# Attention pieces in a fixed TensorE order beside the projections, key norms beside the query projection, adaLN sums by token tile

## The chip, the cores and the metric

The kernel runs on one core of a Trainium2 chip. The metric is the device time of one execution in microseconds (us), as the median over runs. One further execution was taken by the profiler; all views of the profile belong to that one.

## The reference

One layer of a diffusion backbone: 256 latent tokens and 256 context tokens of width 2048, one neighbourhood attention of 16 heads of 128, and a gated ConvFFN of width 5504. Cut to what is computed:

```python
sh1, sc1, g1, sh2, sc2, g2 = adaln(c, w_ada, b_ada)        # silu(c) @ w_ada + b_ada, six vectors of 2048
csh1, csc1, ... = adaln(c_ctx, w_ada, b_ada)
h  = modulate(rms_norm(x,   norm_mix_g), sh1,  sc1)
hc = modulate(rms_norm(ctx, norm_mix_g), csh1, csc1)
q, k, v = split(concat(h, hc) @ w_qkv)                     # q of the latent tokens alone
q, k = rms_norm(q, q_g), rms_norm(k, k_g)                  # per head
p = softmax(q k^T * scale + bias(rpb), masked by window)   # 256 queries x (256 latent + 256 context) keys
x = x + g1 * ((p v) @ w_o)
hf = modulate(rms_norm(x, norm_ffn_g), sh2, sc2)
gate, up = split(dwconv3(hf @ w_up, conv_w, conv_b))
out = x + g2 * ((silu(gate) * up) @ w_down)
```

All inputs are float32. To keep that precision every operand of a large product is split into a high part, rounded to a faster format, and a low part (the rest); a product is then three matmuls: high by high, high by low, low by high.

## The kernel before

**Weights.** Every weight tile is 256 rows by up to 512 columns. `wpair` (line 147) loads it on SP's queue (tile wr, four buffers), casts it on ScalarE into wh (three buffers, line 155) and subtracts on VectorE into wl (two buffers, line 156). `weight` (line 185) keeps two pairs ahead, in the order of one list for the whole kernel.

**First products.** While the first third of adaLN is formed on TensorE, the first keys and the values of groups 0 and 1 are accumulated (`first_products`, line 459).

**The attention phase.** The 16 heads are worked in four groups of four. Projections of 512 columns follow each other: query 0, key 1, query 1, value 2, key 2, query 2, key 3, query 3, value 3. `project` (line 383) takes eight weight pairs; for each it calls `nat` (line 370), which runs over two token tiles (queries) or four (keys and values, which also cover the context), with six matmuls for each token tile. The results stand in the four PSUM banks pj.

Two lists of pieces of work are fed in beside them. `side` holds attention pieces and is ticked after each token tile in `nat` at RATE = 0.46 or RATE3 = 0.36 pieces; `ada` holds the later adaLN parts and is ticked after each weight pair, at 0.44 times the number of token tiles.

- A **score piece** (line 600): three matmuls into a bank, bias add and row maximum on VectorE, exponential on ScalarE, reciprocal on VectorE, scaling on ScalarE. There are two for each head, one for each query tile.
- A **turn** (line 627): four transposes of the probabilities into a bank, cast on ScalarE (high part), subtraction on VectorE (low part).
- A **weigh** (line 641): 12 matmuls of 256 columns with the values, and a copy on ScalarE.
- **Key and query norms** (`norm_transpose`, line 515; `split_k`, `split_q`): for each token tile four squares with sums on ScalarE, a power -0.5 on GpSimd with Newton steps on VectorE (`rsqrt_newton`, line 192), the product on VectorE, four transposes, and a split on ScalarE and VectorE. Keys have four token tiles, queries two. Before, they are traced between a query projection's end and the next key or value projection.
- An **adaLN part** (`ada_tasks`, line 252): a 512 KB load of two 128-row blocks on SP's queue (tile wa, three buffers); five of eight parts are scaled on ScalarE (line 276) and added on GpSimd (line 277), the others are done on VectorE (line 279). After eight parts `finish` (line 283) adds both sums on VectorE, transposes four blocks on TensorE and reduces. There are 12 columns of eight parts in this phase, for g1, sh2 and gs2.

**Order.** Each engine takes its instructions in one fixed order, which a scheduler sets when the kernel is built, from its own model of the times. So TensorE's order is what that model found ready, across projections, attention, norms and adaLN. SP's queue, with all loads, is in order too. The scores, norms and weighings alternate between the bank pairs ms and mx (`at`, line 83); turns use ms alone.

**After it.** The output product (line 740 on) starts with the first 12 heads' rows, with the rest of group 3's attention beside it, then comes the feed-forward part. `xg` there reads the last adaLN columns.

Of the kernel before, what the change touches and what calls it, by code (L numbers as in the profile page):

```python
# [15 lines left out]
P = 128  # L16
# [12 lines left out]
RATE, RATE3 = 0.46, 0.36  # L29
# [21 lines left out]
def block_kernel(  # L51
# [29 lines left out]
    turns = []  # L81
# [47 lines left out]
    rp = cp.tile([NH * NDR, 31], F32, name="rp")  # L129
    nc.scalar.dma_start(rp, rpb)  # L130
# [121 lines left out]
    def ada_tasks(pool, i, c, dst, gcol=None):  # L252
# [29 lines left out]

        def finish():
            acc = st["acc", 0]
            nc.vector.tensor_add(acc, acc, st["acc", 1])
            sp = ms()
            for b in range(4):
                nc.tensor.transpose(sp[:, b * P : (b + 1) * P], acc[:, b * P : (b + 1) * P], ident)
            d = dst[:, 4 * c : 4 * c + 4]
            bc = S_B + i * KD + 4 * c  # L290
            nc.vector.tensor_reduce(
                out=d, in_=sp.rearrange("p (b t) -> p b t", t=P), axis=AX.X, op=ALU.add
            )
# [7 lines left out]
        return [(lambda q=q: load(q), lambda q=q: part(q)) for q in range(KD // KT)], finish  # L301

    def ada_pieces(cols):

        loads = [l for pairs, _ in cols for l, _ in pairs]
        parts = [p for pairs, _ in cols for _, p in pairs]
        n = KD // KT

        def piece(i):
# [5 lines left out]
            if i % n == 1 and i > n:  # L315
                cols[i // n - 1][1]()
            with tc.issue_after(last[0]), tc.issue_after(last[1]):
                if i < len(parts):
                    parts[i]()
                else:  # L320
                    cols[-1][1]()

# [14 lines left out]
    xp = xctx.enter_context(tc.tile_pool(name="xp", bufs=1))  # L337
    s32 = xp.tile([P, KD, 32], F32, name="s32")
# [31 lines left out]
    def nat(psl, tt0, w, kt0, n, first, last):  # L370

        wh, wl = w
        for i, pt in enumerate(psl):
            ts = slice((tt0 + i) * P, (tt0 + i + 1) * P)
            for k in range(n):
                kt = kt0 + k
                a, z = first and k == 0, last and k == n - 1
                nc.tensor.matmul(pt, hh[:, kt, ts], wh[:, k, :], start=a, stop=False)  # L378
                nc.tensor.matmul(pt, hh[:, kt, ts], wl[:, k, :], start=False, stop=False)  # L379
                nc.tensor.matmul(pt, hl(kt, ts), wh[:, k, :], start=False, stop=z)  # L380
# [131 lines left out]
    def row2k(name):  # L512
        return ap.tile([P, CH], F32, tag="r2", name=name, bufs=3)

    def norm_transpose(pt, gcol, dh, dl, t0):

        ss = ap.tile([P, 4], F32, tag="ss", name="ss", bufs=2)
        qn = row2k("qn")
        for h in range(4):
            hc = slice(h * HD, (h + 1) * HD)  # L520
            nc.scalar.activation(qn[:, hc], pt[:, hc], AF.Square, accum_out=ss[:, h : h + 1])
        nc.vector.tensor_scalar(
            out=ss, in0=ss, scalar1=1.0 / HD, scalar2=EPS, op0=ALU.mult, op1=ALU.add
        )
        r = rsqrt_newton(ap, ss, 4, "n")
        nc.vector.tensor_tensor(
            out=qn.rearrange("p (h d) -> p h d", d=HD), in0=pt.rearrange("p (h d) -> p h d", d=HD),
            in1=r.unsqueeze(2).to_broadcast([P, 4, HD]), op=ALU.mult,
        )
        tp = at()  # L530
        for h in range(4):
            nc.tensor.transpose(tp[:, h * P : (h + 1) * P], qn[:, h * HD : (h + 1) * HD], ident)
        tpv = tp.rearrange("p (h t) -> p h t", t=P)
        nc.scalar.activation(dh[:, :, t0 : t0 + P], tpv, AF.Copy, scale=gcol)
        nc.vector.scalar_tensor_tensor(
            out=dl[:, :, t0 : t0 + P], in0=tpv, scalar=gcol,
            in1=dh[:, :, t0 : t0 + P].bitcast(F32), op0=ALU.mult, op1=ALU.subtract,
        )

    def split_k(kps):  # L540
        kh = kv.tile([P, 4, 2 * T], F32R, tag="kh", name="kh")
        kl = kv.tile([P, 4, 2 * T], F32R, tag="kl", name="kl")
        for tt in range(4):
            norm_transpose(kps[tt], kg, kh, kl, tt * P)
        return kh, kl

    def split_q(qps):
        qq = kv.tile([P, 2, 4, T], F32R, tag="qq", name="qq")
        qh, ql = qq[:, 0], qq[:, 1]
        for tt in range(2):  # L550
            norm_transpose(qps[tt], qg, qh, ql, tt * P)
        return qh, ql

    def split_v(vps, g):
        vv = (big, ap)[g % 2 == 0].tile([P, 2, 4, CH], F32R, tag=("vv", "row1")[g % 2], name="vv")
        vh, vl = vv[:, 0], vv[:, 1]
        for tt in range(4):
# [4 lines left out]
        return vh, vl  # L562
# [27 lines left out]
    def attention(g, q, k, v):  # L590

        (qh, ql), (kh, kl) = q, k

        bank = lambda: ms() if late else at()

        def head(h4):
# [3 lines left out]
            def scores(qt):  # L600
                with tc.high_priority():
                    if qt == 0:
# [3 lines left out]
                        st["ph"] = kv.tile([P, 4, T], F32R, tag="pth", name="pth", bufs=2)  # L606
                        st["pl"] = ap.tile([P, 4, T], F32R, tag="ptl", name="ptl", bufs=2)
                    tq = slice(qt * P, (qt + 1) * P)
                    sp = bank()
                    nc.tensor.matmul(sp, qh[:, h4, tq], kh[:, h4, :], start=True, stop=False)  # L610
                    nc.tensor.matmul(sp, qh[:, h4, tq], kl[:, h4, :], start=False, stop=False)
                    nc.tensor.matmul(sp, ql[:, h4, tq], kh[:, h4, :], start=False, stop=True)
# [14 lines left out]
            def turn(qt):  # L627
                tq = slice(qt * P, (qt + 1) * P)
                pr, tp = st[qt], ms()
                for kt in range(4):  # L630
                    nc.tensor.transpose(
                        tp[:, kt * P : (kt + 1) * P], pr[:, kt * P : (kt + 1) * P], ident
                    )
# [7 lines left out]
            def weigh():  # L641
                (vh, vl), ph, pl, op = v[0], st["ph"], st["pl"], bank()
                hc = slice(h4 * HD, (h4 + 1) * HD)
                for kt in range(4):
                    nc.tensor.matmul(
                        op[:, :T], vh[:, kt, hc], ph[:, kt, :], start=(kt == 0), stop=False
                    )
                    nc.tensor.matmul(op[:, :T], vh[:, kt, hc], pl[:, kt, :], start=False, stop=False)
                    nc.tensor.matmul(
                        op[:, :T], vl[:, kt, hc], ph[:, kt, :], start=False, stop=(kt == 3)  # L650
                    )
# [8 lines left out]
        s = [[lambda f=h[0], t=t: f(t) for t in range(2)] for h in heads]  # L660
        t = [[lambda f=h[1], t=t: f(t) for t in range(2)] for h in heads]
        w = [[h[2]] for h in heads]
        seq = s[0] + t[0] + s[1] + t[1]
        if g == 3:
            return [seq, w[0] + s[2] + t[2] + w[1] + s[3] + w[2] + t[3] + w[3]]
        return [seq + w[0] + s[2] + w[1] + t[2] + s[3] + w[2] + t[3] + w[3]]

    cols = [ada_tasks(ap, 2, c, g1T) for c in range(4)]
    cols += [ada_tasks(ap, 3, c, sh2T) for c in range(4)]
    cols += [ada_tasks(ap, 4, c, gs2T, S_GF) for c in range(4)]  # L670
    ada.extend(ada_pieces(cols))

    v, v1 = [[split_v([vsums[g][:, tt, :] for tt in range(4)], g)] for g in range(2)]
    kw, qw = [
# [284 lines left out]
```

## Time and profile before

| what | us |
|---|---|
| median of 3 runs | 1446.48 |
| lowest, highest | 1446.38, 1448.18 |
| the profiled execution | 1445.85 |
| its span, first to last instruction | 1444.0 |

A page of the profile gives the busy time of each engine: PE is TensorE's matmuls, PEld its weight loads, DVE VectorE, ACT ScalarE, POOL GpSimd, SP the queue that issues the loads. A row of a group names the line of the kernel, the engine, what is written from what, the count, the busy us and the mean ns of one, and after the bar the idle time of the engine just before them with what ended it. A row of a timeline has the start in us, the duration, and merged neighbours as "x2" and so on; idle time before it stands in brackets. A row of waits has the total us, how often, and the longest.

### The profile page before, as it was taken

To read this page: it belongs to the slowest core of one execution; us is meant where nothing else is said; L and a number is where in the kernel's file an instruction comes from. 1 tells how busy PE (TensorE), PEld (TensorE's weight loads), DVE (VectorE), ACT (ScalarE), POOL (GpSimd) and SP (SyncE) were. 2 spreads that over 40 slices of the span, in tenths; PEclk is the share of its full clock that TensorE was granted. 3 is DMA by queue.
4 is the path that set the end of the run, shared out by engine and by line. 5 is a ranking of instruction groups with operands and counts; after the bars stand their busy time and mean duration, and the time that the engine had idled before them with its cause. 6 is when DMAs were issued, how large, how long until landed. Compare 5 with 4: busy or idle time off the path is not lost.

```text
span 1444.0 us, 21091 instructions
## 1 busy us (share of the span) xinstructions
PE 1399.1 (97%) x7608; PEld 1167.8 (81%) x7608; DVE 1000.0 (69%) x1541; ACT 778.5 (54%) x1356; POOL 281.1 (19%) x208
## 2 busy tenths in 40 slices
PE   5999999999999999999899999999999999999998
PEld 2666787877787887888788888888888888888888
DVE  4556687686868768756768787887877775545454
ACT  4322265775555675755556566665666654333333
POOL 1000025465445555300101111111111000000000
PEclk9999999999999999999899999999999999999999
DMA  9999548687677677545567777777776666566554
GB/s 308 357 333 313 190 125 269 206 259 218 214 219 254 215 239 232 178 138 189 174 201 224 237 230 242 236 229 234 228 240 196 182 175 206 182 207 204 172 173 156
DMA packets 208920, 317.14 MB, mean 220 GB/s; under 512 B 23360, under 2 KB 87744, under 8 KB 208816
## 3 DMA queue, kind: packets, MB, share of 16 engines
q1 hardware_dynamic: 208688, 315.79, 70.4%
q8 instruction: 59, 0.97, 0.3%
q14 instruction: 45, 0.37, 0.1%
q10 hardware_dynamic: 128, 0.01, 0.0%
HBM read 312.75 MB, written 3.01 MB: 219 GB/s over the span
## 4 chain that ended last, share of the span: by engine, by line
PE 74%; issue 9%; DMA 5%; DVE 4%; ACT 3%; POOL 2%; SPq 1%; DVEq 0%; POOLq 0%; ACTq 0%
PE pj L727 18%; PE pj L733 9%; PE mx L727 8%; PE ms L727 7%; PE pj L379 5%; PE pj L378 5%; PE pj L380 5%; PE mx L733 4%; PE ms L733 4%; DMA wa<-in_w_ada 3%; PE ms L411 2%; PE mx L378 2%; PE mx L379 2%; PE mx L380 2%; POOL acc L277 2%
## 5 line engine op out<-in xcount | busy, mean ns | idle before, releaser
L156 DVE TENSOR_TENSOR wl<-wr,wh 128x1024 fp32r<-128x1024 f32 (+2 forms) x425 | 503.8, 1186 | 280.6 <-PE pj L733 106.3
L155 ACT CAST wh<-wr 128x1024 fp32r<-128x1024 f32 (+2 forms) x425 | 412.1, 971 | 428.8 <-PE pj L727 135.1
L277 POOL TENSOR_TENSOR acc<-acc,wa 128x512 f32<-128x512 f32 x144 | 223.6, 1553 | 428.8 <-issue 260.1
L379 PE MATMUL pj<-wl,hh 128*128 128x512 f32 x512 | 204.7, 400 | 3.5 <-DVE wl L156 3.4
L380 PE MATMUL pj<-wh,hl 128*128 128x512 f32 x512 | 201.7, 397 | 0.0
L378 PE MATMUL pj<-wh,hh 128*128 128x512 f32 x512 | 194.4, 400 | 2.5 <-ACT hh L450 2.5
L727 PE MATMUL pj<-hf,wh 128*128 128x512 f32 x688 | 176.3, 396 | 2.0 <-DVE hf L819 2.0
L727 PEld LDWEIGHTS pj<-hf,wh 128*128 128x128 f32 x688 | 124.9, 191 | 25.1 <-DVE hf L819 2.8
L276 ACT ACTIVATE wa<-wa,sT 128x512 f32<-128x512 f32 x144 | 97.4, 718 | 74.5 <-DMA wa<-in_w_ada 69.3
L379 PEld LDWEIGHTS pj<-wl,hh 128*128 128x128 f32 x512 | 97.7, 191 | 27.2 <-DVE wl L156 6.3
L378 PEld LDWEIGHTS pj<-wh,hh 128*128 128x128 f32 x512 | 96.8, 190 | 26.9 <-issue 3.4
L380 PEld LDWEIGHTS pj<-wh,hl 128*128 128x128 f32 x512 | 97.5, 191 | 19.5
L733 PEld LDWEIGHTS pj<-hf,wl 128*128 128x128 f32 x688 | 94.6, 192 | 6.8
L733 PE MATMUL pj<-hf,wl 128*128 128x256 f32 x688 | 97.8, 285 | 0.0
L727 PE MATMUL mx<-hf,wh 128*128 128x512 f32 x352 | 97.7, 394 | 0.0
L727 PE MATMUL ms<-hf,wh 128*128 128x512 f32 x336 | 90.9, 390 | 0.0
L279 DVE SCALAR_TENSOR_TENSOR acc<-wa,sT,acc 128x512 f32<-128x512 f32 x80 | 73.7, 921 | 6.9 <-DMA wa<-in_w_ada 6.3
L727 PEld LDWEIGHTS ms<-hf,wh 128*128 128x128 f32 x336 | 63.1, 188 | 14.2
L727 PEld LDWEIGHTS mx<-hf,wh 128*128 128x128 f32 x352 | 60.6, 190 | 7.8
L478 DVE TENSOR_TENSOR vsum<-vsum,mx 128x512 f32<-128x512 f32 x64 | 43.2, 684 | 34.2 <-PE mx L380 34.0
L733 PEld LDWEIGHTS mx<-hf,wl 128*128 128x128 f32 x352 | 53.7, 189 | 7.1 <-DVE wl L156 0.4
L584 POOL TENSOR_TENSOR bt<-bt,maskt 128x384 f32<-128x384 f32 x16 | 17.9, 1123 | 206.4 <-DMA bt<-rpd 173.7
(251 smaller groups left out, 2212.0 us busy)
## 6 DMA issues: line engine op xcount, KB each, us to landing
wr<-in_w_up SPq DMA_DIRECT2D x160, 512.0 KB, 4.5
wa<-in_w_ada SPq DMA_DIRECT2D x128, 512.0 KB, 4.6
wr<-in_w_qkv SPq DMA_DIRECT2D x93, 512.0 KB, 4.8
wr<-in_w_down SPq DMA_DIRECT2D x63, 512.0 KB, 4.8
wx<-in_w_ada SPq DMA_DIRECT2D x56, 512.0 KB, 8.6
wr<-in_w_o SPq DMA_DIRECT2D x24, 512.0 KB, 3.9
wr<-in_w_down SPq DMA_DIRECT2D x45, 256.0 KB, 3.0
wr<-in_w_up SPq DMA_DIRECT2D x16, 384.0 KB, 3.4
```

What stands on the lines that cost most here:

```text
L155: a = nc.scalar.copy(hi[:, :kn, :cn], w[:, :kn, :cn])
L156: b = nc.vector.tensor_tensor(out=lo[:, :kn, :cn], in0=w[:, :kn, :cn], in1=hi[:, :kn, :cn].bitcast(F32), op=ALU.subtract,)
L276: nc.scalar.mul(w[:, k, :], w[:, k, :], s)
L277: nc.gpsimd.tensor_add(acc, acc, w[:, k, :])
L279: nc.vector.scalar_tensor_tensor(out=acc, in0=w[:, k, :], scalar=s, in1=acc, op0=ALU.mult, op1=ALU.add)
L378: nc.tensor.matmul(pt, hh[:, kt, ts], wh[:, k, :], start=a, stop=False)
L379: nc.tensor.matmul(pt, hh[:, kt, ts], wl[:, k, :], start=False, stop=False)
L380: nc.tensor.matmul(pt, hl(kt, ts), wh[:, k, :], start=False, stop=z)
L411: nc.tensor.matmul(ap_[32 * k : 32 * k + 32, :n], s32[:, 4 * q + k, :], w[:, k * n : (k + 1) * n], start=(q == 0), stop=(q == 3), tile_pos ...
L478: nc.vector.tensor_add(acc[:, h0 + i, :], acc[:, h0 + i, :], pr_[i])
L727: nc.tensor.matmul(pts[b][:, : t1 - t0], wh[:, k, bs], mov(kt, slice(t0, t1)), start=(kt == 0 and t0 == 0), stop=False,)
L733: nc.tensor.matmul(pts[b][:, :T], wl[:, k, bs], mov(kt, slice(0, T)), start=False, stop=(kt == kn - 1),)
```

## The change

`pin` is new: it ties an instruction behind the one traced before it on its engine, so that the scheduler can't move it. All matmuls and transposes of `nat`, of the attention pieces, of the norms and of adaLN are pinned in this phase; so TensorE's order there is the order of the program text. The other engines' orders are still the scheduler's.

The norms become two kinds of pieces, `norm` (squares to product, in place) and `flip` (transposes and split); the splitting of values becomes pieces too. `project` gets a list of pieces, spreads it evenly over its token tiles, and ends when the list is empty. The lists are written out by hand: S, T and W are scores, turn and weigh, with head and query tile. Key norms and flips stand in the query projection that follows their projection; query norms and flips at the head of the next key or value projection.

The adaLN parts are ticked after each token tile, 0.125 (query projections) or 0.56 of a part, and start after the first query projection. The sum of both halves (`total`) is taken one part after a column's last, its transposes three parts later. Their banks alternate as the others do.

Further: turns use both bank pairs; four row buffers (r2) instead of three; queries of every group are copied out of PSUM into them; the bias table's source `rp` is loaded later, from another pool; the output product's side pieces tick at 512/400 instead of 512/340, and its sum tile `sacc2` takes over a key buffer.

```diff
-RATE, RATE3 = 0.46, 0.36
+ADA_RATE = {2: 0.125, 4: 0.56}
...
+    def pin(ins):
+        if pinned:
+            tc.keep_in_program_order(ins)
...
+        def total():
+            nc.vector.tensor_add(st["acc", 0], st["acc", 0], st["acc", 1])
+
         def finish():
             acc = st["acc", 0]
-            nc.vector.tensor_add(acc, acc, st["acc", 1])
-            sp = ms()
+            sp = bank()
...
             if i % n == 1 and i > n:
                 cols[i // n - 1][1]()
+            if i % n == 4 and i > n:
+                cols[i // n - 1][2]()
...
             side.tick(side.rate)
-    def project(c0, nt):
+            ada.tick(ada.rate)
+
+    def project(c0, nt, pieces=(), lead=0):
         psl = [pj() for _ in range(nt)]
+        side.extend(pieces)
+        for _ in range(lead):
+            side.popleft()()
+        side.rate = len(side) / (nt * (KD // KT))
+        side.credit = 0.5
+        ada.rate = ADA_RATE[nt]
         for kt in range(0, KD, KT):
             nat(psl, 0, weight(w_qkv, kt, KT, c0, CH), kt, KT, kt == 0, kt == KD - KT)
-            ada.tick(0.44 * nt)
+        side.drain()
+        side.rate = ada.rate = 0.0
         return psl
...
-                pr, tp = st[qt], ms()
+                pr, tp = st[qt], bank()
...
+    kn, kt_, k = norms(out_of_psum(kps, kw), kg, k_slots)
+    pieces = mix(v1[:3], kn[:3]) + [v1[3], kt_[0], kn[3]] + kt_[1:]
+    qs = out_of_psum(project(0, 2, pieces))
...
+    ada.extend(ada_pieces(cols))
+    for g in range(4):
+        qn, qt, q = norms(qs, qg, q_slots)
+        heads = attention(g, q, k, values[g])
+        if g == 0:
+            pieces = mix(qn, v0[:2]) + v0[2:] + qt
+        else:
+            pieces = qn + qt
+        c0 = (g + 1) * CH
         if g == 3:
+            pieces += heads("S00 S01 S10 T00 S11 T01 S20 T10 S21 T11")
+            vps = project(2 * D + g * CH, 4, pieces)
+            for piece in split_v(vps, g, values[g]):
+                piece()
+            rest = heads("W0 T20 S30 T21 W1 S31 W2 T30 T31 W3")
+            break
+        pieces += heads("S00 S01 S10 T00 S11 T01 S20 T10 W0 T11 S21 T20 W1 S30")
         if g == 1:
+            n = len(pieces) // 2
+            vps = project(2 * D + c0, 4, pieces[:n])
+            pieces = split_v(vps, 2, values[2]) + pieces[n:]
         if g == 2:
+            kw = big.tile([P, 4, CH], F32, tag="row1", name="kw")
+        kps = project(D + c0, 4, pieces, 5 if g == 1 else 0)
+        kn, kt_, k = norms(out_of_psum(kps, kw), kg, k_slots)
+        a, b = heads("T21 S31 W2 T30"), heads("T31 W3")
+        pieces = mix(kn[:2], a[:2]) + [kn[2], kt_[0], a[2], kn[3], kt_[1], a[3], kt_[2]]
+        pieces += [b[0], kt_[3], b[1]]
+        qs = out_of_psum(project(c0, 2, pieces, 1))
+    pinned.clear()
...
-            tick = (lambda: side.tick(cn / 340)) if i == 0 else (lambda: ada.tick(1.0))
+            tick = (lambda: side.tick(cn / 400)) if i == 0 else (lambda: ada.tick(1.0))
```

More of the change, by code (lines that the diff above doesn't have):

```diff
@@ L512, in row2k @@
     def row2k(name):
[L513 to L538, printed above, removed]
@@ new lines, in block_kernel, with out_of_psum, mix @@
+    kw = oT[:, 8:16, :].rearrange("p (t a) c -> p t (a c)", t=4)
+    def out_of_psum(pts, dst=None):
+        out = [dst[:, tt, :] if dst is not None else row2k("qw") for tt in range(len(pts))]
+        for o, pt in zip(out, pts):
+            nc.scalar.copy(o, pt)
+        return out
+    def mix(*lists):
+        return [p for row in zip(*lists) for p in row]
+    pinned.append(True)
+    values = [{} for _ in range(4)]
+    v0, v1 = [
+        split_v([vsums[g][:, tt, :] for tt in range(4)], g, values[g]) for g in range(2)
+    ]
```

176 lines of the change are left out of this document (88 added, 88 removed).

## The prediction

> **What bounds the kernel now.** I read the page's busy times first, then the windows, then TensorE's timeline where a window lost time, then the waits.
>
> ```profile
> span 1444.0 us, 21091 instructions
> PE 1399.1 (97%) x7608; PEld 1167.8 (81%) x7608; DVE 1000.0 (69%) x1541; ACT 778.5 (54%) x1356; POOL 281.1 (19%) x208
> 193.45:601.00 407.55, 391.40 (x1872) 320.50 (x1871) 308.29 (x466) 256.68 (x537) 207.40 (x143) 0.99 0.73 228
> 300.00:330.00 30.00, 25.54 (x129) 20.60 (x128) 25.57 (x43) 24.23 (x76) 17.60 (x13) 1.00 0.78 243
> 360.00:380.00 20.00, 17.28 (x85) 13.76 (x85) 15.77 (x21) 10.62 (x19) 6.14 (x5) 1.00 0.62 194
> 380.00:436.00 56.00, 56.00 (x281) 47.05 (x280) 40.80 (x58) 34.73 (x75) 26.89 (x21) 1.00 0.73 222
> 436.00:458.00 22.00, 18.81 (x74) 14.56 (x73) 19.82 (x25) 12.69 (x24) 13.50 (x9) 0.84 0.77 251
> 458.00:536.00 78.00, 78.00 (x386) 64.95 (x385) 55.40 (x87) 52.32 (x115) 38.84 (x27) 1.00 0.76 237
> 536.00:557.00 21.00, 18.09 (x86) 14.40 (x85) 18.36 (x32) 15.24 (x46) 15.77 (x11) 0.92 0.71 224
> 557.00:599.00 42.00, 42.00 (x199) 34.80 (x198) 27.36 (x50) 22.00 (x37) 21.42 (x15) 1.00 0.78 236
> ```
>
> Columns of a window: its length, then busy us and instructions of PE, PEld, DVE, ACT and POOL, then TensorE's granted clock, the DMA share and GB/s. TensorE sets the end. The change works in 193.45 to 601 us, from the first query product to the first matmul of the output product. Some windows there are full; four are not (300, 360, 436 and 536), and two of those also show a reduced clock. In them VectorE is busy 79 to 90% of the time, in the full ones 65 to 73%.
>
> Busy time hides part of the loss, because ends of matmuls are modelled. So I price TensorE by the spacing of starts:
>
> ```profile
> 433.93 0.39 PE L378 MATMUL pj<-wh,hh 128*128 128x512 f32 x1
> 434.15 0.39 PE L379 MATMUL pj<-wl,hh 128*128 128x512 f32 x1
> 434.38 0.39 PE L380 MATMUL pj<-wh,hl 128*128 128x512 f32 x1
> 434.61 0.60 PE L532 MATMUL mx<-ident,qn 128*128 128x128 f32 x4
> 434.96 0.71 PE L378 MATMUL pj<-wh,hh 128*128 128x512 f32 x2
> ...
> 316.18 0.28 PE L649 MATMUL ms<-pth,vv 128*128 128x256 f32 x1
> 316.30 0.28 PE L645 MATMUL ms<-pth,vv 128*128 128x256 f32 x1
> ...
> L379 PE MATMUL pj<-wl,hh 128*128 128x512 f32 x448 | 178.9, 399 | 3.5 <-DVE wl L156 3.4
> L631 PE MATMUL ms<-ident,pr 128*128 128x128 f32 x112 | 17.3, 274 | 1.6 <-ACT pr L624 1.4
> L532 PE MATMUL ms<-ident,qn 128*128 128x128 f32 x48 | 7.4, 276 | 4.8 <-DVE qn L526 2.7 <-ACT kh L534 1.3 <-DVE gs2T L291 0.8
> L288 PE MATMUL ms<-ident,acc 128*128 128x128 f32 x48 | 7.3, 274 | 0.0
> L645 PE MATMUL mx<-pth,vv 128*128 128x256 f32 x24 | 7.0, 292 | 2.1 <-ACT pth L635 2.1
> L610 PE MATMUL ms<-kh,qq 128*128 128x512 f32 x14 | 5.8, 418 | 0.1
> L379 PE MATMUL mx<-wl,hh 128*128 128x512 f32 x14 | 5.5, 391 | 0.0
> ```
>
> A 512-column matmul takes 0.227 us of the queue, four transposes 0.355, a 256-column matmul 0.118. Each of the last rows is one of a family of equal rows (projections L378 to L380, scores L610 to L612, weighing L645, L648 and L649, and two banks, ms and mx). So the range holds 3 x 448 = 1344 projection matmuls and 3 x 14 = 42 left from the first products (314 us), 6 x 14 = 84 score matmuls (19), 6 x 24 = 144 of 256 columns (17) and 112 + 96 + 48 = 256 transposes (23): 373 us of 407.55, so **34.2 us are lost**. By the same count the full windows from 380, 458 and 557 lose 0.8, 1.9 and 0.8 us of 176, which is 2%, and the four bad ones 6.2, 3.9, 7.3 and 5.8, together 23.2 of 93. A floor of 2% on 373 is 7.5 us, so at most 34.2 - 7.5 = **26.7 us** can be won.
>
> What the losses are made of:
>
> ```profile
> 449.64 0.63 PE L532 MATMUL ms<-ident,qn 128*128 128x128 f32 x4 [1.14 <-DVE qn L526]
> 451.76 0.79 PE L379 MATMUL pj<-wl,hh 128*128 128x512 f32 x1 [1.50 <-DVE wl L156]
> 452.36 0.63 PE L380 MATMUL pj<-wh,hl 128*128 128x512 f32 x1
> 452.78 0.63 PE L378 MATMUL pj<-wh,hh 128*128 128x512 f32 x1
> ...
> PE mx L532 <- DVE qn L526: 2.5, 2, 1.7
> ```
>
> TensorE's queue is in order; a transpose of normalized keys stands ahead of ready matmuls and waits for the norm. After two waits of at most 1.5 us the spacing is 0.43 us instead of 0.227: the clock has halved. The Trainium skill (TensorE: Matmul & The Clock Gate, section HAM oscillation) asks only for no idle gap over about 3.4 us; this trace halves below that, and the trace decides. Half clock makes 0.16 x 22 + 0.08 x 21 = 5.2 of the bad windows' 23.2 us (22%). By the page the short waits that I leave below would cost no clock, and my sum would be about 2 us lower.
>
> TensorE's waits for norms, keys, probabilities and adaLN are 4.8 + 2.5 + 2.1 + 1.6 = 11.0 us (rows of L532 on ms, L532 on mx, L645, L631); those for weight splits 3.5 (L379). So about 24% of the 23.2 us belongs to splits, **5.6 us**, and the other 17.6 to pieces that stand too close behind what they read.
>
> **The change part by part.**
>
> *Fixed TensorE order.* No matmul is removed; two score groups (6 x 0.227 = 1.4 us) move from the output product into the last value product, which is nothing in the sum. A projection of 4 token tiles has 32 slots of six matmuls (1.36 us), a query projection 16. In the first key projection 22 pieces share 32 slots, 1.45 slots each, so the transpose of head 0 comes three pieces behind its scores, 5.9 us plus two score groups, 7.3 us. What lies between, from the rows below, is a reduce (0.69), a scaling (0.72), an exponential of the same size, a bias add of half of it and small steps: some 3 us bare, and 4 us are left for queues. The tightest is the query transpose in the third key projection: 18 pieces on 32 slots put it after 5 slots, 6.8 us; the norm's ACT, POOL and DVE steps need 4 to 6 us there. I take the 17.6 us as gone; next in line are the splits.
>
> ```profile
> L619 DVE TENSOR_REDUCE nm<-ms 128x1 f32<-128x512 f32 x14 | 9.6, 687 | 0.3
> L624 ACT ACTIVATE pr<-pr,rs 128x512 f32<-128x512 f32 x28 | 19.7, 721 | 5.6 <-DVE rs L623 5.6
> L195 POOL TENSOR_TENSOR nr<-ss,mhalf 128x4 f32<-128x4 f32 x21 | 25.6, 1221 | 28.5 <-DVE ss L522 26.5 <-DVE nt L196 1.0 <-ACT wh L155 0.9
> L156 DVE TENSOR_TENSOR wl<-wr,wh 128x1024 fp32r<-128x1024 f32 x74 | 104.4, 1412 | 20.5 <-PE pj L379 13.6 <-ACT oT L653 2.9 <-ACT wa L276 1.5
> L276 ACT ACTIVATE wa<-wa,sT 128x512 f32<-128x512 f32 x108 | 73.2, 719 | 74.5 <-DMA wa<-in_w_ada 69.3 <-DVE acc L279 1.7 <-POOL acc L277 1.4
> L277 POOL TENSOR_TENSOR acc<-acc,wa 128x512 f32<-128x512 f32 x108 | 166.7, 1543 | 99.5 <-ACT wa L276 53.3 <-DVE acc L274 17.7 <-ACT wh L155 13.5
> 474.42 0.37 SPq L139 DMA_DIRECT2D wa<-in_w_ada  x1
> 495.38 0.37 SPq L139 DMA_DIRECT2D wa<-in_w_ada  x1
> ...
> DMA to landing us min/median/max: 3.5/4.7/8.7
> ```
>
> *Key norms beside the query projection.* Each needs one POOL power (1.22 us); now these queue behind adaLN adds (1.54 each) that wait for loads. In a query projection (21.8 us of matmuls, 27.8 with its pieces) only two adaLN parts remain of seven, so that chain shortens. The query projection's 27.8 us are 96 x 0.227 = 21.8, seven transpose groups (2.5), two weighings of 12 x 0.118 (2.8) and one score group (0.7). In it VectorE has eight splits of 1.41 (11.3 us), twelve passes over 512 columns at some 0.7 by the reduce's row (four norms, four key splits, three probability splits, one score; 8.4) and an estimated 3 of small steps: 23 us, 82%, about what the bad windows have. VectorE's whole work stays 308 us: 76% of the phase now, 78% over 393 us, 81% if all were won. Splits have two buffers, so one can be made only once TensorE has left the one before: a late norm on VectorE delays the next split. I raise the splits' 5.6 us by half to **8.4** (bounds: 2.8 if shorter chains halve it, and 21 if the bad windows' 25% spreads over the 83 us of three query projections).
>
> *adaLN sums by token tile.* 0.25 parts a step in query projections instead of 0.88, 2.24 instead of 1.76 in the others: 17.9 parts in a key or value projection of 48 to 54 us, so one per 2.7 to 3.0 us. Three buffers carry them. The two SP rows are the first and last of 8 loads, spaced 3.0 us while TensorE was full, and ScalarE waited for many of these loads already (69.3 us over the phase). SP is in order, so a load that waits for a buffer holds the next weight load, and a waiting ACT scale holds the next weight cast. The five projections' TensorE work is 5 x 43.6 of matmuls, 27 score groups (18.4), 38 transpose groups (13.5) and 6 weighings (8.5): 258 us, with the floor 264. At 3.0 us a part each wants 53.8 us; the two with 14 and 13 pieces and the one with nine last 48 to 50.5 and fall short by some 9 us together. Half of it can be made up in the query projections, so I take **4 us** (bounds: 0, and the slow rival). The two parts left over run in the output product, which is busy on TensorE.
>
> *At nothing:* squares written to a small tile, products in place and a fourth row buffer (no engine time); two more ScalarE copies of 512 columns, under 0.72 us each, for the third group's queries (ScalarE is 63% busy); transposes over four banks instead of two; the bias table's later load, which has the first products to hide behind. The first query projection can no longer run among the last first products: 0 to 2 us, taken as inside the 4.
>
> Sum: 1445.85 (the profiled execution; span 1444.0 and 1.85 around it) - 26.7 + 8.4 + 4 = 1431.6. The median of the runs is 0.6 above that execution: **1432 us**.
>
> **The rivals.**
>
> *Nearly all is won:* no wait but the 2% floor; 1446.5 - 26.7 = 1420. For it: 78 us in a row at that floor with VectorE at 71%. Against: VectorE must then run at 81%.
>
> *The waits change names:* the order on TensorE is fixed, that on the other engines isn't, so a norm may still come late, or the splits do. With the bad windows' 25% lost over the first query projection and the three later ones (106 us) it is 26 us, the whole gain: 1446, in a band of 1441 to 1449. For it: every window with VectorE over 79% lost time.
>
> *adaLN loads become the bound, slower:* the place is the five key and value projections. If a part takes 3.3 us there (a 4.7 us landing, two scales, two adds, a queue, over three buffers), they last 89.6 x 3.3 = 296 us instead of 264, and these 32 us with 3 of splits outweigh 26.7: 1446.5 + 8.3 = 1455. It decides from (264 + 26.7 - 3) / 89.6 = 3.21 us on. For it: 3.0 us is the densest run of eight loads, and ScalarE waited. Against: TensorE didn't wait in that run.
>
> **How the numbers follow.** Forecast 0.50 (1424 to 1441, which takes the second term from 2.8 to 15), all won 0.17, waits change names 0.13, adaLN bound 0.20. About 0.2%, 3 us, is what a measurement of this kernel can tell from no change. Faster: the first two and a quarter of the third, 0.70; same 0.10; slower 0.20. The range 1419 to 1454 leaves out a third of the all-won case and half of the slow one, under 0.2 in all.
>
> **What would show it.** Right: the key transposes no longer wait for the norm, the reduced clock of the windows from 436 and 536 us is gone, and the phase's TensorE share rises from 96 to 98%. Splits as the first wait of TensorE show the second term. Wrong: key and value projections over 58 us with ScalarE waiting for adaLN loads, or transposes still waiting on norms.

## The result, and the profile after

The changed kernel takes 1458.72 us (median of 4 runs, 1457.09 to 1460.08) beside 1446.57 us of the kernel before: a ratio of 1.0081 [1.0064, 1.0099], some 12 us slower. The forecast was 1432 us, faster, with a range that ended at 1454.

The page of the changed kernel, its span and the first of the busy times (profiled execution 1458.4 us):

```profile
span 1456.6 us, 21052 instructions
PE 1401.7 (96%) x7608; PEld 1171.1 (80%) x7608; DVE 1001.2 (69%) x1541; ACT 785.4 (54%) x1358; POOL 280.6 (19%) x208
```

TensorE has the same 7608 matmuls; of the 12.6 us that the span grew, 10.0 are idle time of TensorE and 2.6 busy time. The windows of the changed kernel, first the whole phase from the first query product to the output product, then six stretches of it (length, then busy us and instructions of PE, PEld, DVE, ACT and POOL, then the granted clock, DMA share, GB/s):

```profile
204.80:614.39 409.59, 386.51 (x1844) 316.92 (x1843) 298.13 (x449) 258.40 (x527) 199.66 (x140) 0.98 0.71 224
...
317.19:366.00 48.81, 48.81 (x229) 40.36 (x228) 35.57 (x51) 26.38 (x53) 28.76 (x20) 1.00 0.77 241
366.00:378.00 12.00, 9.16 (x28) 6.23 (x26) 7.79 (x12) 8.57 (x15) 7.21 (x5) 0.72 0.81 242
378.00:423.00 45.00, 44.80 (x218) 37.46 (x219) 29.64 (x36) 20.25 (x31) 24.61 (x17) 1.00 0.70 228
423.00:436.00 13.00, 7.76 (x28) 6.01 (x27) 7.07 (x15) 10.38 (x28) 6.63 (x6) 0.74 0.81 277
...
558.00:568.00 10.00, 6.15 (x22) 4.77 (x21) 7.54 (x13) 3.13 (x5) 5.63 (x4) 0.83 0.86 265
...
607.00:614.39 7.39, 4.83 (x24) 3.86 (x23) 7.39 (x14) 3.92 (x10) 1.65 (x2) 0.82 0.32 121
```

TensorE's share of the phase fell from 96 to 94% (386.51 of 409.59). It is full for 45 and 49 us in a row and then loses much within 7 to 13 us, at a reduced clock. The four short windows lie where the projection of value 2 ends, where key 2 ends, early in value 3 and at its end. Their clock costs 0.28 x 12 + 0.26 x 13 + 0.17 x 10 + 0.18 x 7.39 = 9.8 us; by the same count the bad windows before cost 5.2. This count takes in the time in which TensorE waits, when a reduced clock costs nothing, so it is an upper bound.

By the prediction's own count (0.227 us a matmul of 512 columns, 0.118 of 256, 0.355 for four transposes) the phase after holds 1344 products (305 us), 90 score matmuls (20), 153 of 256 columns (18) and 256 transposes (23), 366.3 us, and so loses 43.3 us; before it lost 34.2. The other 3.5 us of the span lie in 1.8 us by which the first products end later and 2.4 us of work that now stands ahead of the output product, of which 0.8 is seen again behind it. The same count for each projection, from its first product to the next one's, in us lost (Q, K and V with the group; the prediction's third key projection is K3; the rows add up to 34.4 and 43.6, up to 0.3 from the totals above):

| | Q0 | K1 | Q1 | V2 | K2 | Q2 | K3 | Q3 | V3 |
|---|---|---|---|---|---|---|---|---|---|
| before | 2.8 | 2.5 | 3.4 | 6.9 | 1.7 | 7.5 | 1.2 | 0.8 | 7.6 |
| after | 0.4 | 5.0 | 2.1 | 3.2 | 10.6 | 4.4 | 3.7 | 3.4 | 10.8 |
| length after | 23.6 | 59.0 | 29.9 | 51.9 | 60.8 | 32.2 | 58.1 | 31.6 | 62.7 |

Four places of the kernel before (Q0, Q1, V2, Q2) did gain 10.5 us together; the key projections, Q3 and V3 gave back 19.7, and V3 had lost the most even before. TensorE's waits after (line waited for: us in total, times, longest):

```profile
PE pj L388 <- ACT oT L709: 5.2, 1, 5.2
PE pj L389 <- DVE wl L159: 4.0, 4, 1.2
PE ms L562 <- DVE qw L551: 3.9, 1, 3.9
PE pj L388 <- DVE vv L591: 3.0, 3, 2.1
```

Splits (wl) are a named wait still, but two new ones appeared: the first product into a PSUM bank (L388) waits until the last projection's result has been copied out of it, by ScalarE (L709) or by VectorE after ScalarE (L591). How that comes about shows at 424 us, where K2 ends. TensorE, ScalarE and GpSimd in the timeline of the changed kernel (start, duration, and in brackets the idle time before and what ended it):

```profile
424.26 0.39 PE L390 MATMUL pj<-wh,hl 128*128 128x512 f32 x1
429.89 0.79 PE L388 MATMUL pj<-wh,hh 128*128 128x512 f32 x1 [5.24 <-ACT oT L709]
```

```profile
423.55 1.34 ACT L279 ACTIVATE wa<-wa,sT 128x512 f32<-128x512 f32 x2 [4.34 <-POOL acc L280]
424.79 0.35 ACT L685 COPY oT<-ms 128x256 f32<-128x256 f32 x1
425.04 1.04 ACT L158 CAST wh<-wr 128x1024 fp32r<-128x1024 f32 x1
428.04 1.33 ACT L279 ACTIVATE wa<-wa,sT 128x512 f32<-128x512 f32 x2 [1.95 <-DMA wa<-in_w_ada]
429.28 0.56 ACT L709 COPY oT<-pj 128x512 f32<-128x512 f32 x1
```

```profile
415.63 7.92 POOL L280 TENSOR_TENSOR acc<-acc,wa 128x512 f32<-128x512 f32 x4
```

The products into the old banks are done at about 424.6. ScalarE's queue is in order. A pair of adaLN scalings was held up for 4.34 us behind four GpSimd adds that took 7.92 us, and so pushed a copy and a weight cast back to 426.1; then the next pair waits 1.95 us for its load and takes 1.33, and only behind it, at 429.28, comes the copy that frees the bank. TensorE goes on at 429.89, at half clock (0.79 us instead of 0.39 for the same form). TensorE's row names the copy (ACT oT L709), not the scalings ahead of it; only ScalarE's own timeline shows those.

### The profile page after: what moved, and what is told of

Its sections match the earlier page's. It is cut to its first block, busy times and chain, and to the rows that moved or that the text cites. A ratio compares the mean times of both kernels' runs of the same rounds, so it can differ in the third digit from the quotient of the medians.

```text
span 1456.6 us, 21052 instructions
## 1 busy us (share of the span) xinstructions
PE 1401.7 (96%) x7608; PEld 1171.1 (80%) x7608; DVE 1001.2 (69%) x1541; ACT 785.4 (54%) x1358; POOL 280.6 (19%) x208
## 4 chain that ended last, share of the span: by engine, by line
PE 57%; DMA 2%; DVE 2%; POOL 1%; ACT 1%; issue 1%; DVEq 0%; SPq 0%; ACTq 0%; POOLq 0%
PE pj L775 20%; PE pj L781 10%; PE mx L775 9%; PE ms L775 7%; PE mx L781 5%; PE ms L781 4%; DMA wa<-in_w_ada 2%; POOL acc L280 1%; DVE wl L159 1%; DMA wr<-in_w_down 0%; DVE acc L282 0%; PE ms L680 0%; PE pj L389 0%; PE pj L390 0%; PE pj L388 0%
## 5 line engine op out<-in xcount | busy, mean ns | idle before, releaser
L388 PE MATMUL pj<-wh,hh 128*128 128x512 f32 x512 | 206.5, 409 | 10.7 <-ACT oT L709 5.2
L388 PEld LDWEIGHTS pj<-wh,hh 128*128 128x128 f32 x512 | 97.3, 191 | 35.1 <-ACT oT L709 5.7
L282 DVE SCALAR_TENSOR_TENSOR acc<-wa,sT,acc 128x512 f32<-128x512 f32 x80 | 77.0, 963 | 9.6 <-DMA wa<-in_w_ada 9.2
```

Source lines behind the costliest of these rows:

```text
L282: nc.vector.scalar_tensor_tensor(out=acc, in0=w[:, k, :], scalar=s, in1=acc, op0=ALU.mult, op1=ALU.add)
L388: pin(nc.tensor.matmul(pt, hh[:, kt, ts], wh[:, k, :], start=a, stop=False))
```

## The experiments

Two theories stood against each other at first. **A**: the adaLN sums are too dense in the key and value projections, so that a ScalarE scaling waits for a buffer or a load, and the copies that free the PSUM banks stand behind it. **B**: the fixed order on TensorE itself costs the time, because nothing can pass a late piece. A third, **C**, is that key norms and adaLN can't both stand beside a query projection. Each ratio is to the kernel before, run beside it on the same chip; the losses of the phase are counted as above.

**The order left to the scheduler.** The changed kernel without its pins:

```diff
-    pinned.append(True)
```

> The changed kernel without the pins: the same lists of pieces, but the scheduler orders TensorE again. Theory A (adaLN too dense in key and value projections: a ScalarE scale waits for a buffer or a load, and the copies that free the PSUM banks stand behind it) expects the hand-over waits to stay, since the copies' place on ScalarE doesn't hang on the pins: 1450 to 1460 us. Theory B (the fixed TensorE order itself costs the time, because nothing can pass a late piece) expects the old time or better, 1430 to 1447 us.

Measured: 1450.68 us, 1.0025 [1.0009, 1.0041]. By the ratios the fixed order costs 8 us here. It isn't the whole loss: the phase of the profiled execution still loses 40.5 us, and the bank copies are still among the waits (3.6 us on L591).

**The same adaLN rate in every projection.**

```diff
-ADA_RATE = {2: 0.125, 4: 0.56}
+ADA_RATE = {2: 0.44, 4: 0.44}
```

> The changed kernel with 0.44 of an adaLN part per token tile in every projection, the density of the kernel before (0.88 and 1.76 a weight pair), instead of 0.125 and 0.56. Theory A expects the waits for bank copies and value splits at the ends of value 2 and key 2 (about 8 us with some 7 us of half clock) to go: 1436 to 1446 us. Theory B expects 1455 to 1461. Theory C (key norms and adaLN can't both stand beside a query projection) expects new waits of key transposes there: 1458 to 1466.

Measured: 1448.50 us, 1.0021 [1.0005, 1.0037]; the phase loses 35.5 us. That is beside all three forecasts. Now the query projections lose most (Q2 10.4, Q1 5.8) and splits are the first wait (7.6 us), not key transposes. The loss went to where the adaLN parts went.

**No adaLN sums in the phase, in both kernels.** Both leave the sums of g1, sh2 and gs2 out and set these to ones.

```diff
-    ada.extend(ada_pieces(cols))
+    for dst in (g1T, sh2T, gs2T):
+        nc.vector.memset(dst, 1.0)
```

> The changed kernel with the adaLN sums of the attention phase left out (g1, shift and scale of the feed-forward part are set to 1). Theory A expects the phase to lose only its floor, so 43.6 us of loss fall to 8 to 12, with 4 us of transposes less: 1420 to 1428 us. Theory B expects most of the loss to stay: 1440 us or more.

> The kernel before with the same sums left out, the partner of the run with the changed kernel: the difference of the two is what order and placing of the norms give by themselves. If the fixed order is good in itself, this one is slower than its partner by 3 us or more (its norms' waits stay: 1428 to 1436 us); if the order is what costs, it is faster than its partner.

Measured: 1414.71 us, 0.9784 [0.9759, 0.9810], for the changed kernel, and 1414.02 us, 0.9778 [0.9747, 0.9809], for the kernel before. The phase in the windows, and two groups of the kernel before without adaLN (count | busy us, mean ns | idle before them):

```profile
204.79:574.75 369.96, 369.24 (x1803) 308.29 (x1802) 191.87 (x330) 198.23 (x425) 37.23 (x34) 1.00 0.39 116
```

```profile
195.45:572.76 377.31, 377.31 (x1835) 314.79 (x1835) 202.32 (x346) 194.79 (x429) 39.43 (x35) 1.00 0.39 117
```

```profile
L532 PE MATMUL ms<-ident,qn 128*128 128x128 f32 x48 | 7.5, 273 | 0.0
L532 PE MATMUL mx<-ident,qn 128*128 128x128 f32 x48 | 7.5, 272 | 0.0
```

This decides the question. The second window is the kernel before, with the order and the distances that the prediction blamed: TensorE is busy all of its 377.31 us, at full clock, and by the count of starts its phase loses 6.4 us (7.3 in the changed kernel), about the floor of 2%. The transposes of normalized rows, which waited 4.8 and 2.5 us before, wait 0.0. So the distances suffice when adaLN is gone; the norms were late because of adaLN. Without it the two orders are equal within 0.7 us, less than the intervals. By the ratios adaLN costs 2.2% (32 us) in the kernel before and 3.0% (43 us) in the changed one, and the difference, some 11 us, is nearly the whole change. Its own work on TensorE is 12 columns of four transposes, 4.3 us.

**Which part of adaLN.** The changed kernel with all the arithmetic but only its first three loads of these sums (the later parts use the same data again), and with all the loads but only the first product of each sum (an add of one column for each later one):

```diff
...
+            if n < WA:
+                kept[n] = wload(w_ada, q * KT, KT, i * D + c * CH, CH, pool)
+            st[q] = kept[n % WA]
```

> The changed kernel with every adaLN scale and add of the attention phase kept, but only the first three of their 96 loads: later parts use these three tiles again (so the sums are of other data). If the loads are what is late (landing, buffers, SP's order), the phase falls near its floor: 1416 to 1428 us. If the arithmetic is what costs (GpSimd's and VectorE's shared time, queue places on ScalarE), most of the 44 us stays: 1440 us or more.

```diff
+                if i < 5 and not first:
+                    nc.vector.tensor_add(acc[:, 0:1], acc[:, 0:1], w[:, k, 0:1])
+                    continue
```

> The reverse: every adaLN load of the phase is kept, and of the arithmetic only the first product of each sum; the other blocks get a VectorE add of one column, which reads the tile and so frees its buffer (sums are of one column). If the loads are late by themselves, 1440 us or more; if they are late because ScalarE, GpSimd and VectorE hold the buffers long, 1414 to 1424 us.

Measured: 1436.49 us, 0.9914 [0.9897, 0.9931], without the loads, and 1423.13 us, 0.9822 [0.9803, 0.9840], with the loads alone. Both runs keep the 4.3 us of transposes, so the phase's lost time tells more than the totals: 7.3 us without adaLN, 9.9 with the loads alone, 24.7 with the arithmetic alone, 43.3 with both. The loads alone add 2.6 us, the arithmetic alone 17.4, the two together 36.0, so some 16 us arise only where both are there. A scaling that waits for a load and holds what stands behind it on ScalarE, as at 424 us, needs both; that this makes up all of the 16 isn't shown. TensorE's first waits without the loads:

```profile
PE mx L570 <- DVE ss L554: 4.9, 1, 4.9
PE ms L570 <- DVE qw L559: 2.0, 1, 2.0
```

Those are query norms; K3 loses 8.8 us and V3 7.7. The bank copies are all but gone from the list, so they need the loads; the late norms need only the arithmetic.

One way in which the arithmetic reaches the norms is a slower VectorE. The split of weights and the norm product of queries in the changed kernel, and then without adaLN:

```profile
L159 DVE TENSOR_TENSOR wl<-wr,wh 128x1024 fp32r<-128x1024 f32 x73 | 100.2, 1373 | 18.4 <-PE pj L389 15.7 <-issue 1.7 <-ACT wa L279 0.6
L551 DVE TENSOR_TENSOR qw<-qw,nr 128x512 f32<-128x512 f32 x8 | 8.7, 1098 | 0.1
```

```profile
L159 DVE TENSOR_TENSOR wl<-wr,wh 128x1024 fp32r<-128x1024 f32 x73 | 89.8, 1230 | 59.8 <-PE pj L389 58.9 <-issue 0.6
L551 DVE TENSOR_TENSOR qw<-qw,nr 128x512 f32<-128x512 f32 x8 | 5.6, 702 | 0.3
```

The same product takes 1.10 us on average with GpSimd's adds in the phase and 0.70 without. With the loads alone the two rows stand at 1229 and 702 ns, so it is the arithmetic that slows them. It hangs on when an add runs: in the kernel before, with as many adds, the norm products took 0.69 us, and so did those of keys in the changed one. The Trainium skill (SBUF — State Buffer, section Who interferes with whom) says that a VectorE instruction with two inputs in SBUF contends with a GpSimd instruction that reads SBUF. These rows agree.

**The bank copies first.** In the changed kernel the adaLN parts that fall due in the last two weight pairs of a projection are put off and queued behind the copies on ScalarE:

```diff
...
+            if kt >= KD - 2 * KT:
+                ada.rate = 0.0
...
+        ada.credit += 2 * nt * ADA_RATE[nt]
...
-        for o, pt in zip(out, pts):
-            nc.scalar.copy(o, pt)
+        copies[:] = [nc.scalar.copy(o, pt).ins for o, pt in zip(out, pts)][-1:]
```

> The changed kernel, with the adaLN parts that fall due in the last two weight pairs of a projection put off until after the copies of its banks, and queued behind these on ScalarE. If the order at the hand-over is what costs, the two waits for copies and value splits and the half clock behind them go: 1458.7 - 8 - 8 = 1440 to 1446 us. If adaLN is simply too late everywhere, the waits come back as others: 1452 to 1462.

Measured: 1453.52 us, 1.0029 [1.0015, 1.0043]; the phase loses 33.9 us. TensorE's first waits:

```profile
PE pj L391 <- DVE wl L159: 8.7, 8, 4.0
PE ms L567 <- DVE qw L556: 4.1, 1, 4.1
```

The waits on bank copies are gone, which shows that adaLN parts ahead of the copies caused them; by the ratios that is worth 0.5%, half of what was hoped. Other waits took their place: splits (8.7 us, 4.0 in the changed kernel) and a query norm. That these wait for the parts that were put off and come in a bunch is likely, but no row here shows it.

**Smaller loads, later query flips, another rate.** Three edits of the changed kernel, each alone and together: every adaLN load as two tiles of 256 KB in six buffers of half the size, so that a buffer comes free after one scale and add instead of two; the transposes of the queries of groups 2 and 3 (beside K3 and V3) eight slots of six matmuls later; and 0.50 adaLN parts for each token tile in key and value projections, 0.25 in query ones.

```diff
-            w = pool.tile([P, KT, CH], F32, tag="wa", name="wa", bufs=WA)
+            ws = [pool.tile([P, CH], F32, tag="wa", name="wa", bufs=2 * WA) for _ in range(kn)]
+            for k, w in enumerate(ws):
+                nc.sync.dma_start(w, src[(k0 + k) * P : (k0 + k + 1) * P, c0 : c0 + cn])
...
```

```diff
...
-        side.rate = len(side) / (nt * (KD // KT))
-        side.credit = 0.5
+        side.rate = len(side) / (nt * (KD // KT) - gap)
+        side.credit = 0.5 - gap * side.rate
...
-            vps = project(2 * D + g * CH, 4, pieces)
+            vps = project(2 * D + g * CH, 4, pieces, 2, 8)
...
-        kps = project(D + c0, 4, pieces, 5 if g == 1 else 0)
+        kps = project(D + c0, 4, pieces, (0, 5, 2)[g], 8 * (g == 2))
```

```diff
-ADA_RATE = {2: 0.125, 4: 0.56}
+ADA_RATE = {2: 0.25, 4: 0.50}
```

Smaller loads alone:

> The changed kernel with each adaLN load split into two of 256 KB in tiles of their own, six buffers of half the size in the same memory: a buffer is free after one scale and one add, and the first half lands sooner. If buffers held too long are the cause, 1440 to 1450 us; if not, within 3 us of 1458.7.

Measured: 1446.32 us, 0.9994 [0.9977, 1.0011]: 12 us better than the change as it was. The query projections are near the floor (0.9 to 1.5 us lost), but K3 and V3 still lose 9.3 and 11.7 us, to query norms first:

```profile
PE mx L565 <- DVE qw L554: 5.4, 2, 4.0
PE ms L565 <- DVE qw L554: 3.3, 1, 3.3
```

Later query flips with smaller loads, and the later flips alone:

> The changed kernel with half-size adaLN loads (six buffers) and with the query flips of groups 2 and 3 put 8 slots (11 us) later: their norms start at the head of the projection, the other pieces share the slots that are left. With half loads alone the last key and value projections lost 9.3 and 11.7 us, most of it in query transposes that waited for a norm whose GpSimd power queues behind adaLN adds. If that is the cause, both fall to 3 to 5 us: 1446 - 13 = 1430 to 1437 us, faster than either kernel. If the waits only move to the denser pieces behind, 1442 to 1450.

> The changed kernel with the later query flips alone, full-size loads. The one 4 us wait in the last value projection and its half clock go, the waits for bank copies stay: 1450 to 1455 us. If the buffers' hold isn't a cause beside it, it comes as low as the run with half loads: 1430 to 1437.

Measured: 1439.06 us, 0.9945 [0.9930, 0.9959], together, and 1449.54 us, 1.0018 [0.9997, 1.0039], alone. The flips' waits go in both, and K3 loses 3.6 and 2.3 us. V3 was to fall to 3 to 5 us too and didn't: it loses 7.8 and 8.1, now at its end, where weighings wait for values that are being split (1.6 and 3.2 us at the longest), at half clock. With loads as they were, the bank copies stay:

```profile
PE pj L388 <- DVE vv L591: 5.5, 3, 2.5
...
PE pj L388 <- ACT oT L709: 3.0, 1, 3.0
```

The smaller loads in the kernel before:

> The kernel before with half-size adaLN loads in six buffers, to see whether the gain of half loads is the order's or the loads'. If the loads' hold is a cause in both kernels, 1434 to 1441 us; if it comes only with the denser parts of the change, within 3 us of 1446.5.

Measured: 1444.10 us, 0.9976 [0.9966, 0.9986]. They are worth 0.24% there and 0.87% in the changed kernel (from 1.0081 to 0.9994), where the adaLN parts stand denser in the key and value projections.

The other rate alone, and all three:

> The changed kernel with 0.25 and 0.50 of a part per token tile and nothing else changed. If density alone explains the loss against the kernel before, 1438 to 1446 us; if the buffers and the early query flips hold as much, 1449 to 1456.

> Half loads and later query flips with adaLN at 0.25 and 0.50 of a part per token tile, between the old even 0.44 and the change's 0.125 and 0.56. If the density in key and value projections still costs with half loads, 2 to 5 us below the run with half loads and later flips; if the query projections, with the key norms in them, are the tighter place, 2 to 8 us above it.

Measured: 1449.67 us, 1.0014 [1.0000, 1.0028], for the rate alone, and 1433.41 us, 0.9906 [0.9892, 0.9920], for all three. Against the changed kernel's 1.0081 the loads alone give 0.87%, the flips 0.63% and the rate 0.67%, and the three together 1.75%, a fifth less than their sum: three remedies of about equal worth, not one.

All three with a rate of 0.34 and 0.46, and all three without the pins:

> The fastest version with 0.34 and 0.46 of a part per token tile, one step nearer to the even 0.44. If density in key and value projections is the only thing that counts, faster or the same: 1428 to 1434 us. If query projections with the key norms in them can't take more parts, 1437 to 1444.

> The fastest version (half loads, later query flips, 0.25 and 0.50) without the pins, so that the scheduler orders TensorE again. If the fixed order is worth something once adaLN is paced, slower by 4 us or more: 1437 to 1446. If only adaLN's pacing matters, within 3 us of 1433.4.

Measured: 1431.09 us, 0.9884 [0.9865, 0.9903], and, without the pins, **1428.60 us, 0.9876 [0.9857, 0.9896]**, the lowest here and faster than both kernels. These two can't be told apart by their intervals. The phase of the second and all of TensorE's waits in 195 to 590 us:

```profile
194.00:582.00 388.00, 385.40 (x1883) 320.23 (x1881) 304.09 (x468) 266.83 (x547) 198.62 (x138) 1.00 0.75 238
```

```profile
PE ms L683 <- DVE vv L594: 1.1, 1, 1.1
PE mx L565 <- DVE qw L554: 1.1, 1, 1.1
PE ms L667 <- DVE ptl L672: 0.2, 1, 0.2
```

TensorE is busy 385.40 of 388.00 us at full clock, with VectorE at 78% and GpSimd still busy for 199 us; by the count of starts the phase loses 12.8 us, beside 43.3 in the changed kernel. So nearly the same adaLN work can run beside TensorE at little cost; its size isn't what stops TensorE, but when its loads, scalings and adds come. With the pins the same kernel is 0.3% slower (0.9906 [0.9892, 0.9920], the intervals just overlap), so the fixed order, the headline of the change, buys nothing with adaLN either.

## Why the prediction was wrong, point by point

**What bounds the kernel.** Right: TensorE sets the end, and 34.2 us were lost in the phase. Taking adaLN away brings the phase to its floor and wins 32 us, adaLN's own 4.3 us of TensorE work among them, so some 28 us could be won; the prediction's bound was 26.7.

**The step that failed**: "the other 17.6 to pieces that stand too close behind what they read", and then "I take the 17.6 us as gone". The rows behind it say which tile a transpose waited for, not why that tile was late. The 17.6 us did not go. Of the waits behind them, 11.0 us by name, the changed kernel still has 7.9 (norms 3.9 and 1.0, probabilities 1.2 and 0.8, adaLN transposes 1.0), and 8.2 us on bank copies came new. Distance doesn't rank them either: V3's query transposes stand six slots, 8.2 us, behind the head of their projection and waited 3.9 us, those of K3 stand five slots, 6.8 us, and waited 0.4. The kernel before without adaLN keeps every distance and has no wait of TensorE at all. More distance is a remedy (0.63% for the later flips), but the norms were late because of what adaLN puts beside them.

How, shows in the kernel before at the wait of 1.14 us for a norm at 449.64 us. GpSimd's add, then the norm's chain on VectorE:

```profile
445.43 3.12 POOL L277 TENSOR_TENSOR acc<-acc,wa 128x512 f32<-128x512 f32 x2
```

```profile
445.48 1.25 DVE L196 TENSOR_TENSOR nt<-nr 128x4 f32<-128x4 f32 x1 [0.25 <-POOL nr L195]
446.66 0.74 DVE L279 SCALAR_TENSOR_TENSOR acc<-wa,sT,acc 128x512 f32<-128x512 f32 x1
447.32 1.25 DVE L197 SCALAR_TENSOR_TENSOR nt<-nt,ss 128x4 f32<-128x4 f32 x1
448.60 0.16 DVE L200 SCALAR_TENSOR_TENSOR nr<-nt,nr 128x4 f32<-128x4 f32 x1
448.80 0.69 DVE L526 TENSOR_TENSOR qn<-oT,nr 128x512 f32<-128x512 f32 x1
```

Two steps of four columns take 1.25 us while a GpSimd add runs, where such a step else takes 0.16, and a product of adaLN stands between them. That is 2.2 us on the two steps alone, more than the wait. The other two waits for norms over 1.5 us (1.71 ending at 310.95, 1.53 at 326.34) have such steps too, one of 1.26 us and two of 1.24 and 1.13. GpSimd's own power was not held by an adaLN add in these three (a bias add held the first by 2.4 us); in the changed kernel without loads it was, by 1.3 us ahead of the wait of 4.9. These rows stood in the trace before the change was made. Fixing TensorE's order gives such pieces a fixed place, but it doesn't make what they read come earlier, and an order that can't yield adds waits: 8 us as made, 0.3% in the last version.

**The splits' term** (5.6 us raised to 8.4) was high, but of the right order: splits made TensorE wait 3.5 us before and 4.0 after, which by the prediction's own scale is 6.4. They weren't where the loss grew.

**The adaLN term** was put at 4 us. As measured, adaLN's cost rose from 32 to 43 us, some 11. The sum priced a part by its pace over three buffers and by the query projections' spare room. It named the holds ("a waiting ACT scale holds the next weight cast") but not the worst thing behind such a scale: the copy that frees a PSUM bank, for which TensorE waits with nothing else to do. That is the 5.2 us wait at 424 us. "The tightest is the query transpose in the third key projection" was the right kind of piece, and costed at nothing: in the changed kernel query transposes waited 3.9 us in V3 and 1.0 in K3, and without the loads 4.9 us in K3.

**The rivals.** The slow one came nearest: 1455 for 1458.7, with adaLN in the five key and value projections as its place. Four of them last over 58 us (59.0, 60.8, 58.1, 62.7), as "What would show it" asked of it, and ScalarE waits 67 us for adaLN loads. The five last 292.5 us, where it had said 296. Its mechanism was only half right. It takes a steady pace of 3.3 us a part for the bound. The four long projections come to 3.2 to 3.5 us a part, but V2 took its 17.9 parts in 51.9 us, 2.9 us each, and TensorE was full for 48.8 of these. The loss isn't a steady shortage: it falls at a few moments, where a part that waits stands ahead of a bank copy or a norm. The waits of ScalarE's scale after, then those of SyncE's queue of loads after, and last the same queue before:

```profile
ACT wa L279 <- DMA wa<-in_w_ada: 67.1, 32, 4.8
...
ACT wa L279 <- POOL acc L280: 10.6, 4, 4.3
```

```profile
SPq L142 <- DVE wl L159: 135.0, 50, 7.4
SPq L142 <- POOL acc L280: 129.9, 54, 7.8
```

```profile
SPq L139 <- POOL acc L277: 103.9, 51, 5.8
```

ScalarE waited just as long for loads before (69.3 us), so the sum of that wait says nothing. What grew is ScalarE's wait for GpSimd's adds, from 1.4 to 10.6 us, and that of the loads in SyncE's queue until such an add frees a buffer, from 103.9 to 129.9.

**The clock.** Forecast: the reduced clock goes. It left the windows from 436 and 536 us, came up in others, and grew from 5.2 to 9.8 us. In the window from 366 us the waits are those for vv, the longest 2.1 us; in the one from 423 us there is one of 5.24 us. The Trainium skill (TensorE: Matmul & The Clock Gate, section HAM oscillation) asks only for no gap over about 3.4 us: the second agrees, the first doesn't, nor did the kernel before. Those 4.6 us more of lost clock stand beside 9.1 us more of loss in all: at most half of what the new waits cost came through the clock.

**Range and chances.** The range gave the slow case 0.20 and ended at 1454, 4.7 us short. The chance of 0.70 for faster rested on one reading of a wait that the rows of VectorE and GpSimd, in the four bad windows, could have put in doubt. That the slow rival's total came within 4 us is in part luck, since only some of its path is what happened.

Still open: how the 17 us that the arithmetic alone adds divide between VectorE slowed by GpSimd's adds and places in the queues; what makes up the 16 us that need both loads and arithmetic; whether and why the scheduler's order is 0.3% better than the fixed one in the last version; and which of the changed kernel's other parts that version needs, since the three edits were not tried together on the kernel before.

## What to carry to other kernels

A wait names the tile that was late, not what made it late: before an order is rebuilt around such waits, take the suspected background work out in one run and see whether they go. On in-order engines look at what stands ahead of the copies that free PSUM banks, since a background step that waits there for a load stops TensorE for the whole wait and a drop of the clock besides. Where background work must run, give it small buffers that come free early, a rate that leaves room in every stage, and a gap between a norm and its first reader: here each alone brought under 1% and the three brought 1.75%.

## What the runs showed of the hardware that was not expected

In the phase, loads alone add 2.6 us of lost time and arithmetic alone 17.4, but the two together 36.0: here the waits of two background streams on in-order queues came to nearly twice their sum.

Small VectorE steps suffer most, in proportion, from GpSimd's adds. The step of L200 below takes 322 ns on average in the changed kernel, and 162 without adaLN and 160 with its loads alone. Two of these steps of the changed kernel's norm, 0.7 us apart, in VectorE's timeline:

```profile
559.87 0.16 DVE L200 SCALAR_TENSOR_TENSOR nt<-nt,ss 128x4 f32<-128x4 f32 x1
...
560.61 1.23 DVE L200 SCALAR_TENSOR_TENSOR nt<-nt,ss 128x4 f32<-128x4 f32 x1
561.76 0.27 DVE L203 SCALAR_TENSOR_TENSOR nr<-nt,nr 128x4 f32<-128x4 f32 x2
561.95 3.44 DVE L551 TENSOR_TENSOR qw<-qw,nr 128x512 f32<-128x512 f32 x2
```

The second runs beside GpSimd adds that began at 560.24 us and takes 1.23 us instead of 0.16; the two products after it take 3.44 us together instead of 1.40 (0.702 each without adaLN). That chain, in which a product of adaLN had also waited 0.59 us for its load on VectorE's queue, ended in the 3.9 us wait for qw.
